# A hybrid decoder layer on one core: a second plain feature tile ahead of the block products, and the token sums on VectorE alone

## The chip, the cores and the metric

The kernel runs on one core of a Trainium2 chip. The metric is the device time of one execution in microseconds (us); the kernel before takes 1684.22 us, the median of three runs between 1683.53 and 1684.87. The engines are named as in the profile: PE is TensorE, PEld its weight load, DVE VectorE, ACT ScalarE, POOL GpSimd, and SP the engine whose queue issues the DMAs.

## What is computed

One decoder layer on 1024 tokens of width 1024 (16 learned tokens are put in front and dropped at the end). Three mixers (window attention, forgetting attention, a gated recurrence) are gated, summed and projected; then comes a gated feed-forward part, which is what the change touches:

```python
u = rms_norm(x, norm_ffn)
gate_ff, up_ff = jnp.split(u @ w_ffn_in, 2, axis=-1)      # 1024 x (2 x 2816)
h = x + (jax.nn.silu(gate_ff) * up_ff) @ w_ffn_out        # 2816 x 1024
return rms_norm(h, norm_final)[:, 16:]
```

All of it is float32.

## The kernel before

**Number form.** Every float32 operand of a matmul is held as two tiles, a high part (rounded by ACT, `split`, L118) and the rest (subtracted by DVE, L119). A product is three matmuls: high by high, high by rest, rest by high (`mm3`, L150).

**The feed-forward part** has 22 feature tiles of 128 columns (NF = 22, NJ = 11), taken in pairs j and j + 11. A plain tile (`swiglu_plain`) multiplies its gate and its up weights with both halves of the tokens: 2 x 2 products of 8 contraction steps, each of three matmuls of 512 columns, 96 matmuls. A block tile (`swiglu`) treats gate and up weights by contraction halves as the 2 x 2 blocks a11, a12, a21, a22, and the tokens by contraction and token halves as b11 to b22, and needs seven block products in place of eight, 7 x 12 = 84 matmuls. Their second operands are b11, b21, b22 and four sums of token blocks, t1 to t4, which `combine()` makes once: t2 is the second operand of a block tile's third product, t1 of the fourth, t3 of the fifth, t4 of the seventh. The first and second products need no sum. The first operands are sums of weight blocks, made on POOL (L900, L903) and split by ACT and DVE; the sixth needs such a sum too.

In the kernel before, feature tile 0 is plain and the other 21 are block tiles. PE's order is: plain tile 0; block tile 11; then the pairs 1 and 12, 2 and 13, up to 10 and 21. `combine()` works in pieces of 512 columns: of four pieces k, two are made by DVE and two by POOL (`e = pool if k > 1 else dve`), in tiles of the tag "c". For each pair `combine_w` makes sums of the second weight matrix and `combine_a` sums of the activations, all on POOL, and these are written to device memory.

**The second product** (`product2`) reads these back (tiles "raw"), splits them into "ab" tiles, and forms the 1024 x 1024 result of 7 block products with 11 contraction steps each, 12 matmuls a step. The "ab" tiles are a ring of 15 in one memory pool that lies over memory of the first product.

**Order.** Each engine works through its own list in order. A scheduler of the framework makes these lists from the program: it moves instructions of one engine past each other where the data allow it, and it places a tile when the memory under it is free. A DMA on SP's queue that waits holds up those behind it.

Of the kernel before, what the change touches and what calls it, by code (L numbers as in the profile page):

```python
# [46 lines left out]
def f32(ap):  # L47
    return ap.bitcast(F32)
# [3 lines left out]
def hybrid_block(ctx, tc, h_in, w_in, w_v0, w_v1, w_bd, par, rows, gains, relt, onehot,  # L52
# [852 lines left out]
    with tc.tile_pool(name="r5", bufs=1, side="right", reuse_waits="tile") as r5:  # L905
# [37 lines left out]
        def swiglu(f, w, bb):  # L943

            (a11, a12), (a21, a22) = w
            b11, b21, b22, t1, t2, t3, t4 = bb
            p1, p2, p5 = mm_bank(f"_s{f}"), sc_bank(f"_s{f}"), tr_bank(f"_s{f}")
            g0, g1, u1 = (t5("c", 8) for _ in range(3))
            s0, s1 = (t5("a", 6) for _ in range(2))
            s2 = t5("s2", 2)  # L950
            product(p1, operand(wp, "wh", 2, a11), b11)
            act.activation(g0, p1, AF.Copy)  # L952
            product(p2, operand(wp, "wl", 2, a12), b21)
            add(dve, g0, p2, g0)
            act.activation(s0, g0, AF.Sigmoid)
            dve.tensor_tensor(s0, g0, s0, ALU.mult)
            sub(pool, a21, a11, a21)
            sub(pool, s2, a22, a21)
            product(p1, operand(r5, "ar", 3, s2), t2, False)
            act.activation(g1, p1, AF.Copy)  # L960
            add(pool, a11, s2, a11)
            product(p5, operand(r5, "ar", 3, a11), t1)
            act.activation(u1, p5, AF.Copy)
            product(p1, operand(r5, "ar", 3, a21), t3, False)
            add(dve, u1, p1, u1)
            sub(pool, a12, a12, s2)
            product(p5, operand(wp, "wh", 2, a12), b22, False)
            add(dve, g1, p5, g1)
            act.activation(s1, g1, AF.Sigmoid)
            dve.tensor_tensor(s1, g1, s1, ALU.mult)  # L970
            dve.tensor_tensor(s1, u1, s1, ALU.mult)
            product(p1, operand(wp, "wl", 2, a22), t4, False)
            dve.tensor_tensor(s0, p1, s0, ALU.mult)
            return [s0, s1]

        def combine():

            b11, b21 = u2[0][:2], u2[0][2:]
            b12, b22 = u2[1][:2], u2[1][2:]
            t3 = [pair_tile(r5, bufs=4) for _ in range(2)]  # L980
            t2, t1 = ([pair_tile(mp) for _ in range(2)] for _ in range(2))
            parts = lambda b, k: [f32(x[:, k % 2]) for x in b[k // 2]]
            into = lambda t, k, v: split(*(x[:, k % 2] for x in t[k // 2]), v)
            v2 = {}
            for k in (0, 2, 1, 3):
                e = pool if k > 1 else dve
                v3, v2[k] = t5("c", 8), t5("c", 8)
                for v, x, y in zip((v3, v2[k]), parts(b22, k), parts(b12, k)):
                    sub(e, v, x, y)
                add(e, v3, v3, v2[k])  # L990
                for x, y in zip((v3, v2[k]), parts(b11, k)):
                    add(e, v2[k], x, y)
                into(t2, k, v2[k])
                into(t3, k, v3)
            t4 = [pair_tile(mp) for _ in range(2)]
            for t, b in ((t1, b22), (t4, b21)):
                for k in (0, 2, 1, 3):
                    e = pool if k > 1 else dve
                    v = t5("c", 8)
                    h, l = parts(b, k)  # L1000
                    sub(e, v, h, v2[k])
                    add(e, v, v, l)
                    into(t, k, v)
            return b11, b21, b22, t1, t2, t3, t4

        def spill(i, j, x):
# [2 lines left out]
        def combine_w(j):  # L1009

            raws = []
            for i in range(2):
                raw = t5("fo", 2, D)
                dma(raw, w_fo[(j + NJ * i) * P:(j + NJ * i + 1) * P])
                raws += halves(raw)
            b11, b12, b21, b22 = raws
            t2 = t5("t2", 1)
            sub(pool, b12, b22, b12)
            add(pool, t2, b12, b11)
            sub(pool, b11, b22, t2)  # L1020
# [3 lines left out]

        def combine_a(j, a11, a21, a12, a22):

            s2 = t5("t2", 1)
            spill(1, j, a12)
            spill(6, j, a22)
            sub(pool, a21, a11, a21)  # L1030
# [3 lines left out]
            for i, x in ((2, s2), (3, a11), (4, a21), (5, a12)):  # L1034
                spill(i, j, x)

        for j in range(NJ):
            if j == 0:
                first = swiglu_plain(0)
                ws = fetch_fi(NJ, 0)  # L1040
                bb = combine()
            else:
                first = swiglu(j, fetch_fi(j, 1), bb)
                ws = fetch_fi(j + NJ, 0)
            spill(0, j, first[0])
            combine_w(j)
            combine_a(j, *first, *swiglu(j + NJ, ws, bb))
    ctx4.close()

    with (tc.tile_pool(name="ring", bufs=1, side="right", reuse_waits="tile") as rr,
          tc.tile_pool(name="r6", bufs=1, side="right", reuse_waits="tile") as r6):
        def h_tile(tt, half):
            t = r6.tile([P, 512], F32, name=f"h{tt}{half}")
# [3 lines left out]
        def right_operand(i, j):  # L1059
# [2 lines left out]
            row, half = {0: (j, 0), 1: (j + NJ, 0), 5: (j + NJ, 1)}[i]  # L1062
            return w_fo[row * P:(row + 1) * P, 512 * half:512 * half + 512]

        def operands(i, j):

            raw = wp.tile([P, 2, 512], F32, tag=("wr", "wh", "wl")[j % 3], bufs=2, name=nm("raw"))
            dma(raw[:, 0], asp[i][j])
            dma(raw[:, 1], right_operand(i, j))
            t = rr.tile([P, 2, 2, 512], F32R, tag="ab", bufs=15, name=nm("ab"))  # L1070
            split(t[:, 0], t[:, 1], raw)
            return t[:, 0], t[:, 1]

# [144 lines left out]
```

## Time and profile before

| | |
|---|---|
| median of three runs | 1684.22 us |
| profiled execution, its time | 1683.39 us |
| its span (first to last instruction) | 1681.6 us |
| PE busy | 1628.9 us, 97% |
| DVE busy | 1003.4 us, 60% |
| ACT busy | 766.0 us, 46% |
| POOL busy | 463.8 us, 28% |

PE is the engine that works nearly all the time, so a microsecond counts if PE waits in it, or if its clock is low. The profile tells for each instruction how long the engine had been idle before it and what ended that; a group can be asked for by stretch of time. Times of PE instructions overlap (they are pipelined), so the step from one start to the next is the price of one. "Granted clock" is the share of 2.4 GHz that PE was given: 1.00 is that, 0.50 is 1.2 GHz.

### The profile page before, as it was taken

What the parts mean: (1) busy time and instruction counts of PE and PEld (TensorE: products, weight loads), DVE (VectorE), ACT (ScalarE), POOL (GpSimd) and SP (SyncE); (2) the same over time, 40 slices, a digit from 0 to 9 for tenths busy, and PEclk for the clock granted to TensorE, in tenths of its full rate; (3) what the DMA queues carried; (4) which work ended last, traced back from release to release, by engine and by line L of the source; (5) the groups of instructions that cost most, each with busy time, mean ns of one, the idle gap of its engine ahead of it and who ended that gap; (6) DMA issues with size and microseconds to landing.
All of it is one profiled execution on the core that took longest, in us unless ns stands there. A gap on an engine that the chain in (4) does not pass through costs nothing.

```text
span 1681.6 us, 22693 instructions
## 1 busy us (share of the span) xinstructions
PE 1628.9 (97%) x8147; PEld 1372.5 (82%) x8147; DVE 1003.4 (60%) x1815; ACT 766.0 (46%) x1413; POOL 463.8 (28%) x363
## 2 busy tenths in 40 slices
PE   7999999999999999999999995899999999999998
PEld 6898888888888888888887884688888888788886
DVE  6566566554666667532357448866666666657544
ACT  6455465554556555533345433433333333346342
POOL 2111011011122122100234007666666566300000
PEclk9999999999999999999999998899999999999999
DMA  7122342213413233159645213244444444499532
GB/s 268 55 97 92 138 135 95 96 61 117 126 64 120 83 126 97 62 176 328 197 155 189 100 63 125 98 165 157 165 167 144 145 155 158 149 358 325 192 122 100
DMA packets 110880, 242.48 MB, mean 144 GB/s; under 512 B 11944, under 2 KB 23544, under 8 KB 110512
## 3 DMA queue, kind: packets, MB, share of 16 engines
q1 hardware_dynamic: 110768, 241.04, 42.2%
q8 instruction: 64, 1.05, 0.3%
q14 instruction: 48, 0.39, 0.1%
HBM read 163.45 MB, written 72.21 MB: 140 GB/s over the span
## 4 chain that ended last, share of the span: by engine, by line
PE 80%; DVE 7%; issue 4%; DMA 4%; ACT 3%; POOL 2%; SPq 0%; POOLq 0%; DVEq 0%; ACTq 0%
PE mm_w L150 23%; PE mm_s L150 13%; PE tr_s L150 7%; PE mm_br L150 5%; PE mm_wo L150 5%; PE mm_x L1082 4%; PE sc_s L150 4%; PE ob L547 3%; PE tr L558 3%; PE tr_y L1082 3%; PE sc_y L1082 3%; PE mm_v L150 2%; PE ob_x L1082 1%; PE sc L632 1%; PE sc L633 1%
## 5 line engine op out<-in xcount | busy, mean ns | idle before, releaser
L150 PE MATMUL mm_w<-uh,wh 128*128 128x512 f32 (+2 forms) x744 | 292.6, 393 | 0.0
L150 PE MATMUL mm_w<-uh,wl 128*128 128x512 f32 (+2 forms) x744 | 280.6, 377 | 0.0
L150 PE MATMUL mm_w<-ul,wh 128*128 128x512 f32 (+2 forms) x744 | 280.0, 376 | 0.0
L150 PEld LDWEIGHTS mm_w<-uh,wl 128*128 128x128 f32 x744 | 140.0, 188 | 25.6
L150 PEld LDWEIGHTS mm_w<-uh,wh 128*128 128x128 f32 x744 | 140.5, 189 | 12.8
L150 PEld LDWEIGHTS mm_w<-ul,wh 128*128 128x128 f32 x744 | 140.8, 189 | 11.8
L119 DVE TENSOR_TENSOR ab<-raw,ab 128x1024 fp32r<-128x1024 f32 x77 | 95.9, 1262 | 62.6 <-ACT ab L118 60.2
L150 PE MATMUL mm_s<-pt,ar 128*128 128x512 f32 x504 | 121.3, 389 | 1.7 <-ACT c L952 1.7
L118 ACT ACTIVATE ab<-raw 128x1024 fp32r<-128x1024 f32 x77 | 80.9, 1059 | 88.4 <-DMA raw<-w_fo_dram 29.2
L150 PE MATMUL mm_br<-o,wh 128*128 128x512 f32 x384 | 118.6, 390 | 0.0
L118 ACT ACTIVATE wh<-wr 128x1024 fp32r<-128x1024 f32 (+1 forms) x85 | 71.7, 845 | 97.1 <-PE mm_w L150 50.6
L119 DVE TENSOR_TENSOR pl<-tr,ph 128x384 fp32r<-128x384 f32 (+2 forms) x160 | 87.4, 555 | 47.3 <-ACT ph L118 43.2
L150 PEld LDWEIGHTS mm_s<-pt,ar 128*128 128x128 f32 x504 | 94.5, 188 | 21.6 <-ACT c L952 2.1
L118 ACT ACTIVATE ph<-tr 128x384 fp32r<-128x384 f32 (+2 forms) x160 | 76.9, 486 | 53.1 <-PE tr L558 51.0
L119 DVE TENSOR_TENSOR wl<-wr,wh 128x1024 fp32r<-128x1024 f32 x43 | 53.3, 1239 | 72.2 <-ACT wh L118 71.9
L648 POOL TENSOR_SCALAR s<-s,sm 128x144 f32<-128x144 f32 (+3 forms) x64 | 48.6, 761 | 172.1 <-DVE sm L647 144.1
L150 PEld LDWEIGHTS mm_br<-o,wh 128*128 128x128 f32 x384 | 72.0, 188 | 15.3 <-ACT wh L118 0.3
L150 PE MATMUL mm_s<-pt,wh 128*128 128x512 f32 x252 | 63.4, 401 | 18.6 <-ACT wh L118 12.7
L558 PE MATMUL tr<-ident,s 128*128 128x128 f32 x480 | 79.6, 274 | 1.2 <-POOL s L596 0.6
L150 PE MATMUL mm_wo<-woh,hl 128*128 128x512 f32 x256 | 79.1, 390 | 0.0
L150 PE MATMUL mm_br<-o,wl 128*128 128x512 f32 x192 | 75.3, 392 | 1.8 <-DVE wl L119 1.6
L558 PEld LDWEIGHTS tr<-ident,s 128*128 128x128 f32 x480 | 59.1, 140 | 18.3 <-DVE pl L119 3.4
(256 smaller groups left out, 3715.8 us busy)
## 6 DMA issues: line engine op xcount, KB each, us to landing
wr<-w_in_dram SPq DMA_DIRECT2D x45, 512.0 KB, 3.6
wr<-w_fi_dram SPq DMA_DIRECT2D x44, 512.0 KB, 4.2
raw<-asp SPq DMA_DIRECT2D x77, 256.0 KB, 3.9
asp<-a SPq DMA_DIRECT2D x66, 256.0 KB, 2.9
gz<-z SPq DMA_DIRECT2D x48, 256.0 KB, 2.1
o<-osp SPq DMA_DIRECT2D x24, 512.0 KB, 5.3
sg<-gz SPq DMA_DIRECT2D x48, 256.0 KB, 3.4
fo<-w_fo_dram SPq DMA_DIRECT2D x22, 512.0 KB, 4.3
```

The source lines that it names most:

```text
L118: act.activation(hi, src, AF.Copy)
L119: i = dve.tensor_tensor(lo, src, f32(hi), ALU.subtract)
L150: pe.matmul(ps, a, b, start=first and i == 0, stop=i == n - 1, skip_group_check=not first)
L547: pe.matmul(ob[:, q0:q0 + b - a], vt[:, c], x[:, a:b], start=count == 0, stop=count == n_mm - 1, skip_group_check=True)
L558: pe.transpose(tb[:, col:col + P], src, ident)
L632: pe.matmul(sc[:, :n], qs, kh[:, k0:k0 + n], start=True, stop=False)
L633: pe.matmul(sc[:, :n], qs, kl[:, k0:k0 + n], start=False, stop=True)
L648: pool.tensor_scalar(s[:, :nk], s[:, :nk], den, 1.0, ALU.mult, ALU.mult)
L1082: pe.matmul(banks[x], a[:, 0, q], b[:, 1], start=first and j == 0 and c == 0, stop=j == NJ - 1 and c % 3 == 2, skip_group_check=True)
```

## The change

1. For j = 0 both tiles of the pair, 0 and 11, are plain, and stand ahead of `combine()` in the program. The first block tile is tile 1.
2. `combine()` works on whole tiles of 1024 columns, on DVE alone. Its temporaries take the four slots of "fo" (4 KB each), which the rows of the second weight matrix use later ("fo" had two slots); "c" has six slots, not eight. The sum tile "t2" of `combine_w` and `combine_a` moves from one slot to the two of "z".
3. From j = 1 on, the weights of the first tile of a pair are loaded into the pool "wstream" and those of the second into the pool "r5"; before, it was the other way round.
4. The ring of "ab" tiles becomes two pools: four tiles ("ring0") and ten ("ring1"), 14 in all.

```diff
-            g0, g1, u1 = (t5("c", 8) for _ in range(3))
+            g0, g1, u1 = (t5("c", 6) for _ in range(3))
...
-            for k in (0, 2, 1, 3):
-                e = pool if k > 1 else dve
-                v3, v2[k] = t5("c", 8), t5("c", 8)
-                for v, x, y in zip((v3, v2[k]), parts(b22, k), parts(b12, k)):
-                    sub(e, v, x, y)
-                add(e, v3, v3, v2[k])
-                for x, y in zip((v3, v2[k]), parts(b11, k)):
-                    add(e, v2[k], x, y)
-                into(t2, k, v2[k])
-                into(t3, k, v3)
+            temp = lambda: t5("fo", 4, D).rearrange("p (k t) -> p k t", k=2)
+            v2 = []
+            for i in range(2):
+                v3 = temp()
+                v2.append(temp())
+                for v, x, y in zip((v3, v2[i]), b22[i], b12[i]):
+                    sub(dve, v, f32(x), f32(y))
+                add(dve, v3, v3, v2[i])
+                for x, y in zip((v3, v2[i]), b11[i]):
+                    add(dve, v2[i], x, f32(y))
+                split(*t2[i], v2[i])
+                split(*t3[i], v3)
...
-                for k in (0, 2, 1, 3):
-                    e = pool if k > 1 else dve
-                    v = t5("c", 8)
-                    h, l = parts(b, k)
-                    sub(e, v, h, v2[k])
-                    add(e, v, v, l)
-                    into(t, k, v)
+                for i in range(2):
+                    v = temp()
+                    sub(dve, v, f32(b[i][0]), v2[i])
+                    add(dve, v, v, f32(b[i][1]))
+                    split(*t[i], v)
...
-                first = swiglu_plain(0)
-                ws = fetch_fi(NJ, 0)
+                first, second = swiglu_plain(0), swiglu_plain(NJ)
                 bb = combine()
+                spill(0, j, first[0])
             else:
-                first = swiglu(j, fetch_fi(j, 1), bb)
-                ws = fetch_fi(j + NJ, 0)
-            spill(0, j, first[0])
+                first = swiglu(j, fetch_fi(j, 0), bb)
+                spill(0, j, first[0])
+                second = swiglu(j + NJ, fetch_fi(j + NJ, 1), bb)
             combine_w(j)
-            combine_a(j, *first, *swiglu(j + NJ, ws, bb))
+            combine_a(j, *first, *second)
...
-    with (tc.tile_pool(name="ring", bufs=1, side="right", reuse_waits="tile") as rr,
+    with (tc.tile_pool(name="ring0", bufs=4, side="right", reuse_waits="tile") as r7,
+          tc.tile_pool(name="ring1", bufs=10, side="right", reuse_waits="tile") as r8,
...
-            t = rr.tile([P, 2, 2, 512], F32R, tag="ab", bufs=15, name=nm("ab"))
+            pl = r7 if ring[0] % 14 < 4 else r8
+            ring[0] += 1
+            t = pl.tile([P, 2, 2, 512], F32R, tag="ab", name=nm("ab"))
```

What this does to the engines' lists, at three places.

**DVE, where the first block tile's first operand is split.** "pt" are tiles of tokens and of their sums, "c" and (after) "fo" the temporaries of the sums, "wh" and "wl" first operands of a block tile, "a" the gated result. Before:

```order
L119 TENSOR_TENSOR wh_9988<-wr_9861,wh_9988 128x512
L119 TENSOR_TENSOR pt_9874<-c_9925,pt_9873 128x512
L903 TENSOR_TENSOR c_9935<-c_9935,pt_9358 128x512
L930 TENSOR_TENSOR a_9857<-mm_u_1743_9808,a_9857 128x512
L119 TENSOR_TENSOR pt_9876<-c_9930,pt_9875 128x512
L119 TENSOR_TENSOR pt_9874<-c_9935,pt_9873 128x512
L119 TENSOR_TENSOR pt_9876<-c_9940,pt_9875 128x512
L900 TENSOR_TENSOR c_9945<-pt_8985,c_9878 128x512
L900 TENSOR_TENSOR c_9955<-pt_8985,c_9900 128x512
```

After, the split of "wh" for tile 1 stands here, ahead of the splits of t4:

```order
L900 TENSOR_TENSOR fo_10034<-pt_8987,fo_10005 128x1024
L119 TENSOR_TENSOR pt_9992<-fo_10024,pt_9991 128x1024
L903 TENSOR_TENSOR fo_10034<-fo_10034,pt_8988 128x1024
L929 TENSOR_TENSOR a_9977<-mm_g_1754_9927,a_9977 128x512
L119 TENSOR_TENSOR wh_10077<-wr_10064,wh_10077 128x512
L119 TENSOR_TENSOR pt_10016<-fo_10029,pt_10015 128x1024
L119 TENSOR_TENSOR pt_10018<-fo_10034,pt_10017 128x1024
L119 TENSOR_TENSOR wl_10093<-wr_10064,wl_10093 128x512
L119 TENSOR_TENSOR ar_10113<-s_1795_10076,ar_10113 128x512
```

Before, 13 of DVE's instructions of 512 columns on the sums came after the split of the first "wh". Now only the two splits of t4 do; the other 24 instructions of `combine()`, 1024 columns wide, and the two splits of tile 11's weights stand ahead of it, from the last tiles of the tokens on.

**POOL, from the first weight sum on.** "wr" and "s" are weight blocks and their sums, "fo" and "t" those of the second matrix. Before:

```order
L900 TENSOR_TENSOR wr_9863<-wr_9861,wr_9863 128x512
L900 TENSOR_TENSOR s_1790_9987<-wr_9863 128x512
L900 TENSOR_TENSOR c_9888<-pt_9359,pt_9355 128x512
L900 TENSOR_TENSOR c_9889<-pt_9360,pt_9356 128x512
L903 TENSOR_TENSOR c_9888<-c_9888,c_9889 128x512
L903 TENSOR_TENSOR c_9889<-c_9888,pt_8983 128x512
L900 TENSOR_TENSOR fo_9966<-fo_9968,fo_9966 128x512
L903 TENSOR_TENSOR c_9889<-c_9889,pt_8984 128x512
L903 TENSOR_TENSOR t_1781_9970<-fo_9966 128x512
L900 TENSOR_TENSOR fo_9966<-fo_9968,t_1781_9970 128x512
L900 TENSOR_TENSOR fo_9968<-fo_9968,t_1781_9970 128x512
```

After:

```order
L900 TENSOR_TENSOR wr_10201<-wr_10199,wr_10201 128x512
L900 TENSOR_TENSOR a_9857<-a_9803,a_9857 128x512
L900 TENSOR_TENSOR wr_10066<-wr_10064,wr_10066 128x512
L900 TENSOR_TENSOR s_1795_10076<-wr_10066 128x512
L900 TENSOR_TENSOR s_1813_10211<-wr_10201 128x512
L903 TENSOR_TENSOR wr_10064<-s_1795_10076,wr_10064 128x512
L900 TENSOR_TENSOR fo_10040<-fo_10042,fo_10040 128x512
L903 TENSOR_TENSOR t_1783_10044<-fo_10040 128x512
L900 TENSOR_TENSOR fo_10040<-fo_10042,t_1783_10044 128x512
L900 TENSOR_TENSOR fo_10042<-fo_10042,t_1783_10044 128x512
L900 TENSOR_TENSOR wr_10064<-wr_10064,s_1795_10076 128x512
```

No sum of tokens is left on POOL. Five instructions stand ahead of the addition `wr_10064<-s_1795_10076,wr_10064`, which overwrites a block that the split of "wh" (above) reads.

**ACT, at the end of the first product.** "ab" are operands of the second product; L952 to L969 belong to the last block tile. Before:

```order
L952 ACTIVATE c_12912<-mm_s_2182_12909 128x512
L955 ACTIVATE a_12915<-c_12912 128x512
L960 ACTIVATE c_12913<-mm_s_2182_12909 128x512
L963 ACTIVATE c_12914<-tr_s_2184_12911 128x512
L969 ACTIVATE a_12916<-c_12913 128x512
L118 ACTIVATE ab_13071<-raw_13068 128x1024
```

After:

```order
L952 ACTIVATE c_12843<-mm_s_2165_12840 128x512
L118 ACTIVATE ab_13018<-raw_13015 128x1024
L955 ACTIVATE a_12846<-c_12843 128x512
L118 ACTIVATE ab_13036<-raw_13033 128x1024
L960 ACTIVATE c_12844<-mm_s_2165_12840 128x512
L118 ACTIVATE ab_13054<-raw_13051 128x1024
L118 ACTIVATE ab_13072<-raw_13069 128x1024
L963 ACTIVATE c_12845<-tr_s_2167_12842 128x512
L969 ACTIVATE a_12847<-c_12844 128x512
```

Four "ab" tiles are now rounded among the last block tile's instructions and not behind the last of them; DVE's list has their four subtractions at the same place.

On SP's queue one load per pair moves: the second half of the weights of the next pair's first tile stood ahead of the last write of `combine_a` and of three writes of `combine_w`, and now stands behind them.

## Rows read from the trace of the kernel before

**Rows 1.** Page: PE over the span, and the granted clock in 40 slices.

```profile
PE 1628.9 (97%) x8147; PEld 1372.5 (82%) x8147; DVE 1003.4 (60%) x1815; ACT 766.0 (46%) x1413; POOL 463.8 (28%) x363
PEclk9999999999999999999999998899999999999999
```

**Rows 2.** Three of the four longest waits of PE: total us, times, longest.

```profile
PE mm_s L150 <- ACT wh L118: 12.7, 1, 12.7
...
PE mm_s L150 <- DVE wh L119: 5.9, 1, 5.9
PE sc_s L150 <- DVE wl L119: 5.4, 1, 5.4
```

**Rows 3.** Timeline of PE, 1030 to 1082: start us, us, instruction, idle before.

```profile
1030.70 0.39 PE L150 MATMUL mm_u<-pt,wl 128*128 128x512 f32 x1
1043.84 1.22 PE L150 MATMUL mm_s<-pt,wh 128*128 128x512 f32 x2 [12.74 <-ACT wh L118]
...
1064.03 4.63 PE L150 MATMUL sc_s<-pt,wl 128*128 128x512 f32 x10 [5.40 <-DVE wl L119]
...
1078.94 2.88 PE L150 MATMUL mm_s<-pt,wl 128*128 128x512 f32 x12
1081.66 2.43 PE L150 MATMUL mm_s<-pt,wh 128*128 128x512 f32 x10
```

**Rows 4.** Stretches: length, busy us (count) of PE, PEld, DVE, ACT, POOL; clock; DMA.

```profile
1031.00:1043.90 12.90, 0.16 (x2) 0.07 (x1) 7.42 (x6) 2.42 (x5) 12.66 (x10) 0.63 0.29 101
...
1051.00:1055.20 4.20, 4.20 (x11) 3.33 (x12) 4.20 (x5) 2.63 (x5) 2.92 (x2) 0.54 0.00 0
...
1081.70:1462.00 380.30, 380.30 (x1679) 314.93 (x1678) 245.88 (x275) 140.70 (x236) 232.21 (x153) 1.00 0.46 157
```

**Rows 5.** Timeline of DVE, a split of 1024 columns and the next.

```profile
918.15 1.21 DVE L119 TENSOR_TENSOR wl<-wr,wh 128x1024 fp32r<-128x1024 f32 x1
919.28 0.68 DVE L119 TENSOR_TENSOR hl<-sg,hl 128x512 fp32r<-128x512 f32 x1
```

**Rows 6.** Timeline of DVE, token tiles, sums beside POOL, and splits without it.

```profile
1012.25 1.14 DVE L124 SCALAR_TENSOR_TENSOR pt<-tr,part,pt 128x128 fp32r<-128x128 f32 x3 [1.21 <-ACT pt L123]
...
1020.16 1.77 DVE L119 TENSOR_TENSOR pt<-c,pt 128x512 fp32r<-128x512 f32 x1
1021.86 1.77 DVE L903 TENSOR_TENSOR c<-c,pt 128x512 f32<-128x512 f32 x1
...
1071.70 0.69 DVE L119 TENSOR_TENSOR wl<-wr,wl 128x512 fp32r<-128x512 f32 x1
1072.31 0.69 DVE L119 TENSOR_TENSOR wh<-wr,wh 128x512 fp32r<-128x512 f32 x1
```

**Rows 7.** Timeline of POOL, beside DVE's sums, and while DVE waits.

```profile
1021.35 1.74 POOL L900 TENSOR_TENSOR fo<-fo,fo 128x512 f32<-128x512 f32 x1
...
1036.65 1.26 POOL L903 TENSOR_TENSOR c<-c,c 128x512 f32<-128x512 f32 x1
```

**Rows 8.** Page: splits of 1024 columns, DVE and ACT, mean ns of one.

```profile
L119 DVE TENSOR_TENSOR ab<-raw,ab 128x1024 fp32r<-128x1024 f32 x77 | 95.9, 1262 | 62.6 <-ACT ab L118 60.2
...
L118 ACT ACTIVATE ab<-raw 128x1024 fp32r<-128x1024 f32 x77 | 80.9, 1059 | 88.4 <-DMA raw<-w_fo_dram 29.2
```

**Rows 9.** DMA issues, 940 to 1080: KB each, median us to landing.

```profile
wr<-w_fi_dram SPq DMA_DIRECT2D x4, 512.0 KB, 4.9
```

**Rows 10.** Timeline of PE, start of the second product, and 30 us on.

```profile
1464.83 1.20 PE L1082 MATMUL sc_y<-ab 128*128 128x512 f32 x4 [2.21 <-DVE ab L119]
...
1495.19 2.11 PE L1082 MATMUL mm_x<-ab 128*128 128x512 f32 x8 [0.36 <-DVE ab L119]
```

**Rows 11.** Timeline of DVE at the start of the second product.

```profile
1462.81 8.70 DVE L119 TENSOR_TENSOR ab<-raw,ab 128x1024 fp32r<-128x1024 f32 x5
```

**Rows 12.** Timeline of SP's queue in the first product, one pair of tiles.

```profile
1123.08 0.38 SPq L58 DMA_DIRECT2D wr<-w_fi_dram  x1
...
1129.77 2.02 SPq L58 DMA_DIRECT2D bsp<-fo  x2
```

More of the change, by code (lines that the diff above doesn't have):

```diff
@@ L981, in combine @@
             t2, t1 = ([pair_tile(mp) for _ in range(2)] for _ in range(2))
-            parts = lambda b, k: [f32(x[:, k % 2]) for x in b[k // 2]]
-            into = lambda t, k, v: split(*(x[:, k % 2] for x in t[k // 2]), v)
-            v2 = {}
-            for k in (0, 2, 1, 3):
-                e = pool if k > 1 else dve
-                v3, v2[k] = t5("c", 8), t5("c", 8)
-                for v, x, y in zip((v3, v2[k]), parts(b22, k), parts(b12, k)):
-                    sub(e, v, x, y)
-                add(e, v3, v3, v2[k])
-                for x, y in zip((v3, v2[k]), parts(b11, k)):
-                    add(e, v2[k], x, y)
-                into(t2, k, v2[k])
-                into(t3, k, v3)
+            temp = lambda: t5("fo", 4, D).rearrange("p (k t) -> p k t", k=2)
[10 more added lines that the diff above has]
+                split(*t3[i], v3)
             t4 = [pair_tile(mp) for _ in range(2)]
             for t, b in ((t1, b22), (t4, b21)):
-                for k in (0, 2, 1, 3):
-                    e = pool if k > 1 else dve
-                    v = t5("c", 8)
-                    h, l = parts(b, k)
-                    sub(e, v, h, v2[k])
-                    add(e, v, v, l)
-                    into(t, k, v)
+                for i in range(2):
[3 more added lines that the diff above has]
+                    split(*t[i], v)
             return b11, b21, b22, t1, t2, t3, t4
@@ L1012, in combine_w @@
             for i in range(2):
-                raw = t5("fo", 2, D)
+                raw = t5("fo", 4, D)
                 dma(raw, w_fo[(j + NJ * i) * P:(j + NJ * i + 1) * P])
@@ L1016, in combine_w @@
             b11, b12, b21, b22 = raws
-            t2 = t5("t2", 1)
+            t2 = zp.tile([P, 512], F32, tag="z", bufs=2, name=nm("t2"))
             sub(pool, b12, b22, b12)
@@ L1025, in combine_a @@
         def combine_a(j, a11, a21, a12, a22):
-            s2 = t5("t2", 1)
+            s2 = zp.tile([P, 512], F32, tag="z", bufs=2, name=nm("t2"))
             spill(1, j, a12)
@@ L1063, in right_operand @@
             return w_fo[row * P:(row + 1) * P, 512 * half:512 * half + 512]
+        ring = [0]
         def operands(i, j):
```

## Prediction

> **What bounds the kernel now.** I read the page first: PE is busy for 97% of the span [rows 1], so a gain can come only from PE's waits, from a low clock, or from fewer matmuls. The granted clock falls below full in the 25th and 26th of the 40 slices [rows 1], 1009 to 1093 us. The list of PE's waits [rows 2] names three long ones there, 12.7, 5.9 and 5.4 us, all for first operands of a block tile. The timeline [rows 3] shows where: the plain tile's last matmul starts at 1030.70, and the next tile, a block tile, only gets going at 1064. In the hole the clock falls to half and stays there for a while: the matmuls of 1051.0 to 1055.2 have a granted 0.54 [rows 4], and the ten from 1064.03 on take 4.63 us [rows 3]. What holds PE up is the making of the token sums: POOL is busy for 12.66 of the 12.90 us of the first wait [rows 4], and DVE's list has the sums ahead of the splits that PE wants.
>
> After that PE runs without a wait to 1462 us, 380.30 of 380.30 us busy at full clock [rows 4]. There it waits once more, 2.2 us, for the first "ab" of the second product, and 0.4 us at 1495 [rows 10].
>
> **Part 1: the second plain tile takes the place of a block tile.** A block product of 12 matmuls takes 2.72 us (1078.94 to 1081.66 [rows 3]), so a matmul is 0.227 us. The plain tile 0 ends at 1030.70 + 0.23 = 1030.93. In the kernel before, block tile 11 ends at 1081.66, where tile 1 starts [rows 3]: 50.7 us for a tile whose 84 matmuls are worth 19.0 us. The other 31.7 us are waits and half clock. Now plain tile 11 takes 96 x 0.227 = 21.8 us, to 1052.7, if its weights are there, and the 20 block tiles behind it are the same as before. So the change gives 50.7 - 21.8 = 28.9 us, less what tile 1 now waits, G.
>
> The weights of tile 11: its gate weights go into the slots of tile 0's, which PE reads last at 1025.5 (one product of 24 matmuls before the end). ACT takes 1.06 and DVE 1.13 us more [rows 5, 8], so they are there at 1027.9, and the up weights, by the same count from 1030.9, at 1033.6. PE wants them at 1030.9 and 1036.4. About 3 us of cover each, which the two POOL instructions in that stretch (priced below) don't use up: nothing.
>
> **Part 2: when tile 1 can start.** Its first product needs no sum, only its split "wh", but that stands on DVE behind 24 of the 26 instructions of the sums. DVE begins with the last token tiles at 1012.25 [rows 6]. Up to "wh" come 8 token splits at 0.35 us (three take 1.14, ends overlapping [rows 6]), 26 instructions of 1024 columns (24 of sums, 2 of weights) at 1.13 (918.15 to 919.28 [rows 5]), 7 gate products of 512 at 0.60 (the step of 512 columns without POOL [rows 6]) and "wh" itself at 0.60: 2.8 + 29.4 + 4.2 + 0.6 = 37.0. With 0.5 us of waiting in between (DVE reaches the up product of tile 0's first half before PE has ended it, at 1020.3) "wh" would be ready at 1049.8, 2.9 us ahead of PE's 1052.7.
>
> POOL takes this away. Beside POOL, a DVE instruction with both operands in SBUF takes a step of 1.70 and not 0.60 (1020.16 to 1021.86 [rows 6]), and POOL's own go to 1.74 us, where one needs 1.26 while DVE waits [rows 7]: the two take turns, and each POOL instruction costs DVE 1.10 us. Five stand ahead of "wh" on POOL (order above), and the sixth waits for "wh". The third to fifth need the second half of tile 1's weights, whose load stands on SP behind the write of POOL's second; by a load's 4.9 us [rows 9] they run at about 1041 to 1046, well ahead of "wh". So 5 x 1.10 = 5.5, less 0.5 that falls into DVE's own wait: "wh" at 1054.8, and PE waits 2.1 us.
>
> The second product's "wl" comes behind t4's two splits: 1054.8 + 2 x 1.13 + 0.6 = 1057.7, against PE's 1054.8 + 2.7 = 1057.5. With one or two POOL instructions in between (+1.1 or 2.2) the wait is 1.3 to 2.4; I take 1.7, nearer to one, since POOL must wait for the load of its next. From the third product on PE needs one split in 2.72 us, which DVE makes in 1.7 even beside POOL; the sixth waits for a POOL sum behind the four of the second matrix, 5 x 1.7 = 8.5 us after their load lands at about 1057, then ACT and DVE: 1068 against PE's 1070. G = 3.8 us. Neither wait is longer than the 2.2 us before the second product [rows 10], after which the matmuls ran at full clock; so none is added for the clock.
>
> The bounds of G: below, 0 (POOL's instructions fall where DVE waits). Above: each POOL instruction costs its whole 1.74 [rows 7], and a wide one on DVE its mean of 1.26 [rows 8], 5 x 1.74 + 26 x 0.13 = 12.1, "wh" at 1061.9, a wait of 9.2; the clock then falls as before, ten matmuls at 0.42 (4.2 us [rows 4]) and not 0.227, + 2.0; and 2.4 for "wl": 13.6. I take a value near the lower rows since the step of 1.70 was read in the same kind of instructions.
>
> The Trainium skill's page "SBUF — State Buffer", section "Who interferes with whom", says that a VectorE instruction with two SBUF inputs and a GpSimd instruction that reads SBUF block each other by an exclusive lock for the whole instruction. The rows show the blocking, at 1.10 us; with POOL's whole 1.26 in its place G would be 0.8 higher. The page "Perfetto Trace Analysis", section "Optimizing Scalar/DVE Operations", says that breaking instructions up can help where VectorE is not saturated but makes others wait, which speaks against sums of 1024 columns. Here a wide one costs 1.13 against 2 x 0.60, so going back to halves would cost DVE 26 x 0.07 = 1.8 us, and the plain tile covers the later start.
>
> **Part 3: the second product's start.** The first "ab" were split behind the last block tile's last instruction, from 1462.81 on, five in 8.70 us [rows 11]; now the order has four of them among that tile's instructions, the first behind L952, which reads the tile's first product, 6 x 2.72 = 16 us before its end. So the 2.2 us go. What is late next is the fifth, behind the last block tile's end as the first was; it is wanted 4 x 2.72 = 10.9 us later. The 0.4 us at 1495 may stay: the loads there are issued in the same order. I take 2.4, between 0 (the loads come no earlier) and 2.6. A ring of 14 in place of 15 still holds 14 x 2.72 = 38 us of work: nothing. "c" with six slots holds two block tiles: nothing.
>
> **The sum.** Against the profiled execution: 1683.4 - 28.9 + 3.8 - 2.4 = 1655.9; its time is 0.8 us under the median of the runs, so **1656.7**.
>
> **Rivals.**
>
> *DVE becomes the bound.* The upper bound of G, 13.6, or a second block tile that waits too, since the DVE work that POOL had is now all in one list: 1656.7 + 9.8 = 1666.5, and up to 1675 with one more wait of that size. For it: DVE has no idle time in the list of part 2 beyond 0.5 us. Against it: PE gives DVE 21.8 us more than before. Chance 12%.
>
> *The first product starves later, and the kernel is slower.* On SP's queue one load of 512 KB per pair moves behind four writes: from 1123.08 to about 1131.8 [rows 12], 8.7 us later. It is for tile 3, which begins four tiles of 7 x 2.72 = 19.0 us after 1081.66, at 1157.8, and is wanted first in its third product, at 1163. Landing (4.9 [rows 9]), two POOL sums (3.5), ACT and DVE (2.5) bring 1131.8 to 1143, so some 19 us are left. It decides only from 19 us of further delay, if the four slots of "fo" hold the queue up as well. Each pair would then wait; at 4 us for ten pairs, 1656.7 + 40 = 1697. Chance 4%.
>
> *The sums end last all the same.* If the scheduler's order left tile 1 behind all of the sums, G would be some 5 and the time 1658; that is inside the forecast's range, and the order shows that only t4 is behind.
>
> **How the numbers follow.** Forecast (1651.5 to 1663): 82%. DVE the bound (1663 to 1676): 12%. Starving (above 1687): 4%. No clear difference: 2%. The range: below, G = 0 and the whole 2.6 give 1652.7, and 1 us for the spread of the runs; above, the upper bound of G: **1651.5 to 1666.5**. About 0.2%, 3.4 us, is what a measurement of this kernel can tell from no change: faster 94%, same 2%, slower 4%.
>
> **What would show it.** Right: PE without a wait from 1008 to about 1052.7, a clock of 1.00 there, tile 1's first matmul at 1054 to 1057, one more wait of 1 to 2.5 us for "wl", none from then on; the second product's first matmuls without a wait. Wrong: waits in tile 11 for its weights; a wait as long as the 5.4 us before, with matmuls at half clock after it; waits of PE in any later block tile; no POOL at work beside DVE before 1050, which would put G at 0.

## The result and the profile after

The changed kernel takes 1662.65 us (median of four runs, 1662.29 to 1663.59) against 1684.55 (1683.53 to 1685.96): a ratio of 0.987, 95% interval 0.9853 to 0.9887. The forecast of 1656.7 had the direction and the place; the time lies inside its range and 6.0 us above the forecast. Below are PE and its granted clock, and PE's three waits in the changed part (us in total, times, longest), which answer [rows 1] and [rows 2]. The profiled execution has a span of 1660.5 us and took 1662.29.

```profile
PE 1630.2 (98%) x8159; PEld 1375.1 (83%) x8159; DVE 999.4 (60%) x1799; ACT 760.7 (46%) x1397; POOL 433.1 (26%) x341
PEclk9999999999999999999999999899999999999999
```

```profile
PE mm_s L150 <- ACT c L952: 3.7, 1, 3.7
PE sc_s L150 <- DVE wl L119: 2.0, 1, 2.0
...
PE mm_s L150 <- DVE wh L119: 0.9, 1, 0.9
```

One of the two low slices is gone, the waits of 12.7, 5.9 and 5.4 us too. There are shorter ones for the same two first operands, and one of 3.7 us for ACT's copy L952. That kind is not new: in the kernel before, PE waited 1.66 us for the same copy in tile 11 (its timeline):

```profile
1057.89 0.73 PE L150 MATMUL mm_s<-pt,ar 128*128 128x512 f32 x2 [1.66 <-ACT c L952]
```

The timeline of PE, from the end of tile 11 to the start of tile 12 (answers [rows 3]), and then the stretches (length, busy us of PE, PEld, DVE, ACT, POOL, granted clock; they answer [rows 4]):

```profile
1052.82 0.61 PE L150 MATMUL mm_s<-pt,wh 128*128 128x512 f32 x2
1054.33 2.56 PE L150 MATMUL mm_s<-pt,wh 128*128 128x512 f32 x10 [0.90 <-DVE wh L119]
1056.73 0.61 PE L150 MATMUL sc_s<-pt,wl 128*128 128x512 f32 x2
1059.37 3.57 PE L150 MATMUL sc_s<-pt,wl 128*128 128x512 f32 x10 [2.02 <-DVE wl L119]
1066.68 4.96 PE L150 MATMUL mm_s<-pt,ar 128*128 128x512 f32 x12 [3.75 <-ACT c L952]
1071.48 2.88 PE L150 MATMUL tr_s<-pt,ar 128*128 128x512 f32 x12
...
1082.36 2.88 PE L150 MATMUL mm_s<-pt,wh 128*128 128x512 f32 x12
```

```profile
1031.00:1052.80 21.80, 21.80 (x97) 18.05 (x97) 21.23 (x18) 8.29 (x11) 12.98 (x4) 1.00 0.24 82
...
1061.00:1062.80 1.80, 1.80 (x5) 1.00 (x3) 1.80 (x4) 0.00 (x0) 1.80 (x2) 0.50 0.38 146
1062.80:1066.70 3.90, 0.15 (x2) 0.02 (x1) 2.08 (x2) 1.18 (x3) 3.90 (x3) 0.50 0.70 269
1066.70:1071.50 4.80, 4.80 (x13) 3.80 (x14) 4.80 (x5) 1.21 (x3) 4.09 (x4) 0.56 0.40 157
...
1082.00:1441.00 359.00, 359.00 (x1586) 297.26 (x1585) 244.97 (x264) 135.57 (x225) 217.33 (x145) 1.00 0.46 161
```

Tile 11 runs without a wait at full clock, and from 1082 to 1441 PE is busy all the time. Tile 1 takes 1082.36 - 1052.82 = 29.54 us for 84 matmuls worth 19.04: G is **10.5**, not 3.8. It is the wait for "wh" (the first product takes 1.2 us too long), 2.0 for "wl", 3.75 for L952, and 3.5 of half clock (1.4 in the second product, 2.1 in the third, which takes 4.80 us and not 2.72). The second product of the layer begins without a wait (answers [rows 10]; before, then after):

```profile
1462.00 0.61 PE L1082 MATMUL sc_y<-ab 128*128 128x512 f32 x2
...
1444.12 1.52 PE L1086 MATMUL sc_y<-ab 128*128 128x512 f32 x6
```

So 1462.00 - 1444.12 = 17.9 us, all at the tiles 11 and 1, and 3.2 behind it make the 21.1 us between the spans of 1681.6 and 1660.5.

Why ACT was late with L952: the timelines of ACT and then of POOL (start us, us, instruction, idle before).

```profile
1057.65 0.61 ACT L118 ACTIVATE wl<-wr 128x512 fp32r<-128x512 f32 x1
1065.52 0.63 ACT L118 ACTIVATE wh<-wr 128x512 fp32r<-128x512 f32 x1 [7.25 <-POOL wr L900]
1066.05 0.58 ACT L952 ACTIVATE c<-mm_s 128x512 f32<-128x512 f32 x1
```

```profile
1033.42 6.74 POOL L900 TENSOR_TENSOR a<-a,a 128x512 f32<-128x512 f32 x1 [16.69 <-DVE a L930]
...
1054.49 2.07 POOL L903 TENSOR_TENSOR wr<-s,wr 128x512 f32<-128x512 f32 x1 [3.64 <-ACT pt L118]
1056.52 2.25 POOL L900 TENSOR_TENSOR fo<-fo,fo 128x512 f32<-128x512 f32 x1
1058.84 1.61 POOL L903 TENSOR_TENSOR t<-fo 128x512 f32<-128x512 f32 x1
1060.54 3.28 POOL L900 TENSOR_TENSOR fo<-fo,t 128x512 f32<-128x512 f32 x2
1063.78 1.71 POOL L900 TENSOR_TENSOR wr<-wr,s 128x512 f32<-128x512 f32 x1
```

The third product adds to the bank of the first, so it must wait until L952 has copied the first one out. The bank had been full since 1057. But on ACT's list the rounding of the sixth first operand stands ahead of L952, and that waited 7.25 us for POOL, which made the four sums of `combine_w(0)` first. PE was held up by an operand that it would want three products later.

### The profile page after: what moved, and what is told of

Read it like the earlier page. It is cut to its first block, busy times and chain, and to the rows that moved or that the text cites. A ratio compares the mean times of both kernels' runs of the same rounds, so it can differ in the third digit from the quotient of the medians.

```text
span 1660.5 us, 22597 instructions
## 1 busy us (share of the span) xinstructions
PE 1630.2 (98%) x8159; PEld 1375.1 (83%) x8159; DVE 999.4 (60%) x1799; ACT 760.7 (46%) x1397; POOL 433.1 (26%) x341
## 4 chain that ended last, share of the span: by engine, by line
PE 87%; DVE 4%; issue 4%; ACT 2%; POOL 1%; DMA 1%; SPq 0%; DVEq 0%; POOLq 0%; ACTq 0%
PE mm_w L150 26%; PE mm_s L150 13%; PE tr_s L150 7%; PE mm_br L150 6%; PE mm_wo L150 5%; PE mm_x L1086 4%; PE tr_y L1086 4%; PE sc_y L1086 4%; PE ob L547 3%; PE sc_s L150 3%; PE tr L558 3%; PE mm_v L150 2%; PE ob_x L1086 1%; PE mm_g L150 1%; PE mm_u L150 1%
## 5 line engine op out<-in xcount | busy, mean ns | idle before, releaser
L150 PEld LDWEIGHTS mm_w<-uh,wh 128*128 128x128 f32 x744 | 140.4, 189 | 12.7
L118 ACT ACTIVATE ab<-raw 128x1024 fp32r<-128x1024 f32 x77 | 80.9, 1059 | 94.7 <-PE ob_x L1086 23.4
L150 PE MATMUL mm_s<-pt,ar 128*128 128x512 f32 x480 | 117.4, 394 | 3.7 <-ACT c L952 3.7
L1086 PE MATMUL mm_x<-ab 128*128 128x512 f32 x297 | 72.7, 389 | 0.0
```

What stands on the lines that cost most here:

```text
L118: act.activation(hi, src, AF.Copy)
L150: pe.matmul(ps, a, b, start=first and i == 0, stop=i == n - 1, skip_group_check=not first)
L1086: pe.matmul(banks[x], a[:, 0, q], b[:, 1], start=first and j == 0 and c == 0, stop=j == NJ - 1 and c % 3 == 2, skip_group_check=True)
```

## The experiments

Times are medians of four or five runs. "Tile 1" is the time from tile 1's first matmul to tile 12's, worth 19.0 us.

| kernel | time us | ratio to before, 95% | tile 1 | waits of PE behind tile 1 |
|---|---|---|---|---|
| changed | 1662.65 | 0.9853 to 0.9887 | 29.5 | none |
| e1 sixth operand later | 1662.23 | 0.9849 to 0.9878 | 25.2 | 2.4 in tile 12 |
| e2 combine_w(0) later | 1660.35 | 0.9838 to 0.9867 | 27.3 | none |
| e8 t4 later | 1664.55 | 0.9863 to 0.9896 | 25.1 | 4.1 in tile 12 |
| e10 sum first | 1662.52 | 0.9855 to 0.9884 | 28.0 | 0.6 |
| e6 half width | 1664.19 | 0.9864 to 0.9893 | 31.8 | none |
| e12 eight POOL sums later | 1666.88 | 0.9878 to 0.9911 | 23.0 | 9.0 in tile 12 |
| e11 the same and DVE's order | 1660.84 | 0.9842 to 0.9871 | 19.3 | 1.9 and 3.6 in tile 12 |
| e14 POOL's sums spread | **1651.33** | 0.9790 to 0.9817 | 19.5 | none |
| e15 the same without DVE's order | 1656.05 | 0.9819 to 0.9846 | 23.0 | none |
| e3 one ring | 1666.16 | 0.9877 to 0.9907 | | |
| e4 old sums | 1672.76 | 0.9914 to 0.9943 | | |
| e5 one plain tile | 1671.04 | 0.9903 to 0.9936 | | |

### What each part is worth: each undone alone

```diff
# e3: the ab tiles in one pool again
+            t = rr.tile([P, 2, 2, 512], F32R, tag="ab", bufs=15, name=nm("ab"))
# e4: combine() as before the change, "c" with 8 slots, "fo" with 2
# e5: tile 11 a block tile
-                first, second = swiglu_plain(0), swiglu_plain(NJ)
+                first = swiglu_plain(0)
+                ws = fetch_fi(NJ, 1)
                 bb = combine()
                 spill(0, j, first[0])
+                second = swiglu(NJ, ws, bb)
```

> The changed kernel, with the ring of ab tiles of the second product in one pool of 15 as before (part 3 of the sum undone), all else as changed. Theory A (the own slots for four of them are what took the wait at the start of the second product): PE waits 2.2 us again for the first ab there, and 0.4 us some 30 us later: 1665.0 to 1665.6, 2.4 to 2.9 above the changed kernel. Theory B (the loads come earlier in any case because the slots of the first product's pools are freed in another order): within 0.7 us of the changed kernel.

> The changed kernel with two plain tiles, but combine() as before: pieces of 512 columns, two by DVE and two by POOL, in tiles of the tag c. Theory A (who makes the sums hardly matters once a second plain tile covers them): the time is within 3 us of the changed kernel, 1660 to 1665.5. Theory B (POOL's half is the late half, and POOL's own sums for the weights stand behind it): tile 1's third to fifth operands come later than 1066, PE waits some 4 to 10 us more in tile 1, 1666 to 1673.

> The changed kernel with one plain tile, so that tile 11 is a block tile behind tile 0 as before, but with the sums on DVE alone in instructions of 1024 columns. Theory A (the second plain tile is the gain, since it fills the time that the sums take): PE waits from 1031 to about 1052 for wh, and tile 11 ends where tile 1 ends in the changed kernel, so the time is one block tile above it, 1662.6 + 19.0 = 1681.7 (1678 to 1685). Theory B (the quicker sums are a good part of the gain by themselves): 1672 or less.

Measured: +3.5, +10.1 and +8.4 us, together 22.0, as much as the change brought (21.9). No single one is "the" change. That they are independent is not shown: no run undoes two of them, nor the exchange of the two weight pools alone. Theory A held for the ring: its waits of 2.2 and 0.4 us are back, though the time is 0.6 us above its range. For the other two it fell, and the times lie in theory B's ranges. But with the old sums PE loses its time in another place than B said: the second plain tile itself is held up. Its weights' rounding stands on ACT behind a wait of 11.17 us for POOL's half of the sums, and PE waits 11.9 us in tile 11. Tile 1 starts 19.2 us later (1072.02) and then needs 21.0 us, not 29.5 (waits of PE, then ACT, with the old sums):

```profile
PE mm_g L150 <- ACT wh L118: 11.9, 1, 11.9
```

```profile
1037.40 1.15 ACT L118 ACTIVATE pt<-c 128x512 fp32r<-128x512 f32 x2 [11.17 <-POOL c L903]
...
1042.63 1.04 ACT L118 ACTIVATE wh<-wr 128x1024 fp32r<-128x1024 f32 x1
```

With one plain tile, "wh" was ready at 1042.6 and not at 1054, since tile 11's weights and gate products were not on DVE's list, 20 and not 24 instructions of the sums stood ahead of it, and POOL got no instruction in between (last section). My 1681.7 had carried the changed kernel's 1054 over to a kernel with another list.

### The wait in tile 1: four changes of order

```diff
# e1 (and in e8, e10): the sixth operand behind the copy L963
+                with tc.issue_after(u1_copy.ins):
+                    sixth = operand(wp, "wh", 2, a12)
# e2 (and in e10): combine_w(0) behind tile 12
-            combine_w(j)
+            if j:
+                combine_w(j)
             combine_a(j, *first, *second)
+            if j == 1:
+                combine_w(0)
# e8: the splits of t4 behind tile 1's fifth operand in the program
# e10: besides, on DVE the sum of the first two products ahead of
#      the splits of t4, the seventh operand and tile 12's first two
```

> Only tile 1's sixth first operand is split later: its rounding on ACT and its subtraction on DVE now stand behind the copy of the fourth product (L963), so that on ACT's list the copy of p1 (L952), for which PE waited 3.75 us, no longer stands behind a rounding that waits 7.25 us for POOL. Theory A (ACT's order cost the wait): the third product starts right behind the second, at about 1062.5 in place of 1066.68, the sixth operand is there in time (POOL's sum ends at 1065.5, wanted at about 1071), and the time falls by 3.75 to 6 us, to 1656.7 to 1659; the more, the more of the half clock goes too. Theory B (the half clock lasts to about 1071.5 whatever PE does): PE works in the 3.75 us, but at half clock, so that it gains half of that, 1.9 us: 1660.8. Theory C (DVE and POOL are late anyway, the wait goes to the fourth or fifth operand): less than 1.5 us, 1661.5 or more, with PE's waits now on DVE at L119.

> The sums of the second weight matrix for pair 0 (combine_w(0), four POOL instructions, two loads, four writes) are made behind tile 12 and not behind combine(); the order of ACT is that of the changed kernel. POOL then makes tile 1's sixth sum three instructions earlier, at about 1060.5 and not at 1065.5. Theory A (the wait of 3.75 us is ACT's, and ACT's is POOL's order): L952 runs at about 1061, PE's 3.75 us are gone, 1656.7 to 1659 as with the other order; the split wl of tile 1 may come 1 us earlier as well, since fewer POOL instructions are at work beside DVE. Theory B (half clock to about 1071.5 whatever PE does): 1660.8. Theory C (the four sums are missed elsewhere): PE waits at a later tile, or at the second product, and the time is 1662 or more.

> The sixth operand of tile 1 is split later, as in the first of these runs, and on DVE the two splits of t4, which only the seventh product reads, stand behind the operands of tile 1's third (one of them) and fifth product (the other), not ahead of its second operand; wl is then ready at about 1056 and not at 1059.3. Theory A (what tile 1 loses is the order of the lists, and the clock falls only because PE waits): the wait of 2.0 us for wl and that of 3.75 us go, only the one for wh, some 1.2 us, stays, and the clock stays at 1.00: G falls from 10.5 to 1 to 3, the time to 1652.5 to 1655.5. Theory B (the clock falls behind the plain tiles whatever waits follow): as much wait goes, but some ten us of matmuls at half clock cost up to 3.3 us: 1656 to 1658. Theory C (DVE as a whole is late, so whatever stands behind waits in its turn): the wait goes to the fourth to seventh product, 1659 or more.

> Five moves of order together, no work left out. On DVE, tile 1's first four operands (five splits in all) come first, then the sum of its first two products (the add behind L952), and only then the two splits of t4, the seventh operand and tile 12's first ones; on ACT the sixth operand stands behind the copy of the fourth product; the sums of the second weight matrix for pair 0 are made behind tile 12. Theory A (in the runs before, each freed wait came back because the next copy of p1, L960, stood on ACT behind the sigmoid L955, which waits for DVE's late add; nothing else is late): PE waits only for wh, 1.2 us, the third product starts at about 1059.5, the fifth at about 1065, tile 12 at about 1073.5, and the clock stays at 1.00: 1652.5 to 1655. Theory B (DVE and POOL together have more to do between 1050 and 1085 than PE's work there takes, so that the wait goes on to tile 12, as it did in two of the runs before): PE waits 2 to 5 us in tile 12 or in tile 1's seventh product, 1657 to 1662.

What was to move moved, every time, and most or all of the gain was given back one step on. In e1 the third product starts at 1061.49 and not at 1066.68, and tile 1 is 4.4 us shorter; but the scheduler, with one operand later, also put a weight sum of tile 12 behind other sums on POOL. ACT then waited 11.89 us for it, with L952 of tile 12 behind that, and PE 2.4 us, then twelve matmuls largely at half clock (a step of 4.45 us and not 2.72). The timeline of ACT in e1:

```profile
1081.53 0.63 ACT L118 ACTIVATE ar<-wr 128x512 fp32r<-128x512 f32 x1 [11.89 <-POOL wr L903]
```

In e2 the next copy of the bank was late: ACT (timeline) has the sigmoid L955 ahead of L960, and that waits for DVE's sum of the first two products.

```profile
1069.07 0.63 ACT L955 ACTIVATE a<-c 128x512 f32<-128x512 f32 x1 [5.77 <-DVE c L903]
1069.61 0.58 ACT L960 ACTIVATE c<-mm_s 128x512 f32<-128x512 f32 x1
```

In e8 it is the same wait, 2.87 us, with another of 4.05 us in tile 12 as in e1, and in e10, where that sum came first, the sixth operand's split on DVE, 5.52 us. So theory A, one instruction in the wrong place, fell. The times of e1 and e8 lie in theory C's ranges. That of e2 is near B's 1660.8, but without B's mechanism, since the clock was 1.00 until 1070; e10 is 0.5 us above B's range.

Two causes took the gain back. In tile 1 of e2, e8 and e10 it was DVE's time: in e10 it worked from 1050.5 to 1075.1 with a single gap of 0.15 us, and from 1055 on most instructions with two operands in SBUF took a step of 1.7 us, while POOL worked beside it (timeline of DVE in e10, the sixth operand's split behind these):

```profile
1067.13 3.44 DVE L119 TENSOR_TENSOR wl<-wr,wl 128x512 fp32r<-128x512 f32 x2
1070.50 1.74 DVE L119 TENSOR_TENSOR ar<-s,ar 128x512 fp32r<-128x512 f32 x1
```

In tile 12 of e1 and e8 it was POOL's list, through ACT's: from 1075 to 1080 DVE was idle in both runs. A different order of the same work only chose which product waits.

### Is it the width of 1024?

```diff
# e6: each sum and split of combine() in two pieces of 512, on DVE
+                    for k in range(2):
+                        sub(dve, h(v, k), f32(h(b[i][0], k)), h(v2[i], k))
```

> The sums are on DVE alone as in the changed kernel, but in instructions of 512 columns and not 1024, twice as many. Theory A (back-to-back wide instructions with both operands in SBUF keep POOL out, narrow ones let it in by turns): POOL's first instruction of this stretch, which took 6.74 us, takes 1.7 us or less, the write and the load behind it on SP's queue are issued some 5 us earlier (about 1035.5, not 1040.6), and DVE pays 1.1 us for it and for each of the three that now run earlier. DVE has 26 x 0.07 = 1.8 us more to do; wh comes at 1055 to 1058 and PE waits 2 to 5 us for it and not 1.2. Time: 1661 to 1666. Theory B (the number of instructions with SBUF operands, not their width, keeps POOL out): it takes 6 us or more again, the load is as late, and the time is 1664 to 1667.

No: POOL's instruction took 6.43 us again, in place of 6.74. "wh" came at 1057.3 and PE waited 3.8 us for it, then 4.2 us for the next copy of the bank (L960). The time, 1.5 us above the changed kernel, lies in both theories' ranges and differs by less than its uncertainty; the 6.43 us speak for theory B.

### POOL's sums paid later

```diff
# e12: tile 12's seven operands made ahead (prepare), then
+                    with tc.issue_after(last.ins):
+                        combine_w(0)
+                        combine_a(0, *plain)
# e11: besides, DVE's order as in e10, the sixth operand only behind the sum
# e14: as e11, but combine_w(0) behind pair 6, and for pairs 1 to 3
+                if 2 <= j <= 4:
+                    with tc.issue_after(last_sum[j].ins):
+                        combine_w(j - 1)
# e15: as e14, with DVE's and ACT's lists for tile 1 as in the changed kernel
```

> Only POOL's eight sums are put behind the last weight sum of tile 12; the lists of DVE and ACT are those of the changed kernel. Theory A (POOL's order is behind both the wait of ACT and DVE's slow steps): the wait of 2.0 us for wl stays, since the two splits of t4 still stand ahead of it, though it may shrink by 1.1 us; the one of 3.75 us goes, and the fifth product does not wait either: 1655 to 1659. Theory B (the order of DVE's list is what counts, as the sum of the first two products stands behind six splits there): the wait comes back for the fifth product, as in the run with the second matrix's sums moved: 1659.5 to 1662.

> POOL's sums that are not urgent (combine_a(0) and combine_w(0), eight instructions) are made behind the last weight sum of tile 12, and on DVE tile 1's operands and the sum of its first two products stand ahead of the splits of t4 and of tile 12's operands. Theory A (DVE has too much to do between 1050 and 1075 because nearly each of its instructions runs beside one of POOL, at a step of 1.7 and not 0.6; what POOL can do later must be later): with seven or eight POOL instructions fewer before 1070 DVE has some 8 us in hand, the sixth operand is there at about 1060, and nothing waits behind wh: 1651.5 to 1655.5. POOL's weight sums also come earlier, since the write that held up the load of tile 1's second half is gone from ahead of it. Theory B (POOL finds other work to do beside DVE, so that DVE's steps stay at 1.7, or the eight sums are missed by the writes and loads behind them on SP's queue): waits in tile 12 or in the pair behind it, 1658 or more.

> As the run with all orders, in which tile 1 lost nothing (12 products between 1053.46 and 1075.51 at full clock) but tiles 12 and 2 waited 1.95 and 3.61 us and ran some five us at half clock, because POOL's weight sums for tile 2 came behind eight others, at 1083.5 to 1087.3. Here POOL makes only combine_a(0) ahead of tile 2's weight sums; the sums of the second matrix for pairs 1, 2 and 3 come behind tile 2's, 3's and 4's last weight sum, and those for pair 0 behind pair 6. Theory A (POOL's own list is the last debt of the start, some 14 us of sums that may be paid later since POOL is busy for only 62% of the stretch from 1100 to 1440): no wait of more than 1 us from 1053 on, the clock stays at 1.00, and some 8.7 us less than that run: 1651 to 1654. Theory B (the debt is paid at the next place: tile 2, 13 or 3, or at the start of the second product, where sums of the second matrix come later): 1656 or more.

> POOL's sums are spread as in the run that waits no more, but the lists of DVE and ACT for tile 1 are those of the changed kernel (the splits of t4 ahead of wl, the sixth operand's rounding ahead of the copy of p1, six splits ahead of the sum of the first two products). Theory A (the order on DVE has a price of its own): as in the run with POOL's eight sums moved alone, PE waits 1.9 us for the copy of p1 and runs the third product at half clock (4.44 and not 2.72 us), and nothing waits behind that: 1651.3 + 3.6 = 1654.9, between 1653.5 and 1656.5. Theory B (POOL's order alone is enough): 1652.5 or less. Theory C (both are needed, the debt comes back at tile 12 or 2): 1658 or more.

In e11 tile 1 lost nothing: its operands were split mostly at a step of 0.6 us. But the eight POOL sums stood ahead of tile 2's weight sums, and tile 12 waited for them through the same list of ACT (timeline of ACT in e11; L970 and L972 are tile 12's copies):

```profile
1081.14 0.60 ACT L970 ACTIVATE c<-mm_s 128x512 f32<-128x512 f32 x1 [0.80 <-PE mm_s L150]
1087.33 0.63 ACT L118 ACTIVATE ar<-s 128x512 fp32r<-128x512 f32 x1 [5.58 <-POOL s L900]
1087.86 0.58 ACT L972 ACTIVATE c<-tr_s 128x512 f32<-128x512 f32 x1
```

In e12, without DVE's order, the same debt cost 9.0 us in tile 12, and its 1666.88 lies above the ranges of both theories. In e14 POOL pays it over six pairs, and theory A held: 1651.33, inside its 1651 to 1654. The stretches of e14:

```profile
1031.00:1053.00 22.00, 22.00 (x99) 18.03 (x97) 22.00 (x21) 7.33 (x10) 6.88 (x4) 1.00 0.25 82
1053.00:1100.00 47.00, 47.00 (x207) 38.59 (x206) 39.15 (x40) 20.72 (x35) 34.63 (x23) 1.00 0.44 152
1100.00:1440.00 340.00, 340.00 (x1501) 281.53 (x1500) 227.57 (x246) 124.72 (x207) 213.73 (x142) 1.00 0.49 173
1440.00:1500.00 60.00, 60.00 (x266) 49.70 (x265) 44.56 (x46) 37.66 (x42) 0.00 (x0) 1.00 0.96 340
```

PE does not wait from 1031 to 1500, and its clock stays up. That is 11.3 us below the changed kernel and 33.0 below the one before, and G is about 0.4. Without DVE's order (e15) PE waits 1.90 us for the copy of the bank and runs the third product at half clock (4.39 us): 1656.05, where theory A had 1653.5 to 1656.5. So POOL's order alone brings 6.6 us, and DVE's and ACT's order on top of it 4.7. Tile 1 shows 6.5 and 3.5 of these; the rest of the 4.7 lies ahead of it, where e14 reaches tile 1 at 1051.75 and e15 at 1054.00, and is not explained. The orders on DVE and ACT without POOL's sums spread give 0.1 (e10) and 1.8 us (e11) against the changed kernel. But against e12, from which e11 differs by these orders alone, they give 6.0: what one order is worth depends on the others.

## Why the prediction was right, and where it failed

- **The second plain tile, 50.7 - 21.8 = 28.9 us:** right, and 0.45 us too large. Tile 11 ends at 1052.8 (forecast 1052.7), at full clock, its weights in time. But the 50.7 us of the kernel before hold two matmuls of tile 1, which ran inside tile 11; [rows 3] has ten and not twelve from 1081.66 on. The timeline of before:

```profile
1068.46 0.66 PE L150 MATMUL mm_s<-pt,wh 128*128 128x512 f32 x2
```

- **Small sums:** 1025.5 + 1.06 + 1.13 is 1027.7 and not 1027.9, and from 1030.9 it is 1033.1 and not 1033.6. The weights of tile 11 came at 1028.7 and 1034.5, still ahead of PE. The cover of tile 3's load is 20 us by the prediction's own figures, not 19.
- **When "wh" and "wl" are ready:** right in the end points, 1054.28 (1054.8) and 1059.32 (about 1059, from 1057.5 + 1.7). The way there was different: three of the five POOL instructions fell at 1044.5 to 1050.9, not 1041 to 1046, because the second of the five took 6.74 us and held up the write and the load behind it on SP's queue (1040.56, where 1041 less a load's 4.9 gives about 1036):

```profile
1040.19 0.33 SPq L58 DMA_DIRECT2D asp<-a  x1
1040.56 0.43 SPq L58 DMA_DIRECT2D wr<-w_fi_dram  x1
```

- **The step that failed:** "From the third product on PE needs one split in 2.72 us, which DVE makes in 1.7 even beside POOL". The splits were indeed there: the third operand's at 1061.0. But I asked only when a product's operands are ready and not when its bank is free. The bank is copied by ACT, in ACT's order, behind a rounding that waits for POOL: 3.75 us. The order that I had read shows it; I had read it for DVE and POOL and not for ACT. The trace of before had the same wait, 1.66 us long, and I passed over it.
- **"so none is added for the clock":** wrong, 3.5 us. I argued from one wait of 2.2 us with full clock behind it [rows 10]. Here two waits, 0.9 and 2.0 us, 5 us apart, came ahead of a fall to 0.50. In e15 a single wait of 1.90 us did.
- **G = 3.8:** so mis-sized by 3.75 + 3.5 less 0.6 on the first two waits; it measured 10.5, inside the bounds of 0 and 13.6, which is why the range held. That was luck in part: the upper bound was made of 9.2 us for "wh" (1.2 came), 2.0 for the clock and 2.4 for "wl", and the wait for the bank stood in none of these.
- **The second product's start, 2.4:** the waits of 2.2 and 0.4 us are gone, and what lies behind its first matmul is 3.2 us shorter. With G 6.7 us too small and 0.45 too much for tile 11, that makes the 6.4 us between the 1655.9 of the sum and the profiled 1662.29. Undone alone the ring costs 3.5 us by the medians and 3.1 by the spans. The 0.36 us at 1495 [rows 10], which "may stay", went as well.
- **The rivals:** "DVE becomes the bound" was the nearest: its mechanism, the list that had lost POOL's help, is what e10 shows, though it stayed in one tile. The time is 0.35 us below the 1663 at which that rival's band begins. "Starves later" did not happen: 359.00 of 359.00 us busy behind tile 1.
- **The Trainium skill's page "SBUF — State Buffer", section "Who interferes with whom":** the blocking that it states decided more than the 0.8 us that I gave it, in the other direction too: POOL, and not only DVE, was kept waiting, for 6.74 us in one instruction.
- **The Trainium skill's page "Perfetto Trace Analysis", section "Optimizing Scalar/DVE Operations":** its advice is for an engine that is not saturated. DVE was busy for 21.23 of the 21.80 us of tile 11, and broken into halves (e6) the sums gained nothing.

## What to carry to other kernels

For each product ask three things, when its operands are ready, when its bank is free, and what stands ahead of the instruction that frees it on that engine's list; a rounding that waits for a slow engine, placed early, blocks the copy behind it. When a start-up is overloaded, moving a wait shows the next one: find work of the slow engines that nobody wants soon and spread it over the stretch where they have slack, and read the lists of all engines again after each move, since a scheduler moves other instructions too. Measure the parts of a change by undoing each alone, and do not take their sum for a proof that they are independent.

## What the runs showed of the hardware

**POOL can be kept out for a long time.** In the kernel before, DVE and POOL took turns at 1.70 us. Here a single POOL instruction took 6.74 us (the write of its result was issued at 1040.19, right behind its end), while DVE ran two-operand instructions in SBUF at their undisturbed step of 1.13. It ended when DVE had come to one that reads a PSUM bank (L929). In halves of 512 columns (e6) it is the same, with L929 at 1037.82 (timelines of the changed kernel's DVE, then e6's POOL):

```profile
1036.65 1.23 DVE L903 TENSOR_TENSOR fo<-fo,pt 128x1024 f32<-128x1024 f32 x1
1037.79 1.23 DVE L119 TENSOR_TENSOR pt<-fo,pt 128x1024 fp32r<-128x1024 f32 x1
1038.92 0.69 DVE L929 TENSOR_TENSOR a<-mm_g,a 128x512 f32<-128x512 f32 x1
```

```profile
1032.63 6.43 POOL L900 TENSOR_TENSOR a<-a,a 128x512 f32<-128x512 f32 x1 [15.86 <-DVE a L930]
```

With one plain tile it took 13.62 us, and DVE's step was 1.13 throughout (timelines of e5: POOL, then DVE):

```profile
1034.16 13.62 POOL L900 TENSOR_TENSOR a<-a,a 128x512 f32<-128x512 f32 x1 [13.18 <-DVE a L930]
1047.74 1.29 POOL L903 TENSOR_TENSOR wr<-s,wr 128x512 f32<-128x512 f32 x1
```

```profile
1044.82 1.22 DVE L900 TENSOR_TENSOR fo<-pt,fo 128x1024 f32<-128x1024 f32 x1
1045.95 0.68 DVE L119 TENSOR_TENSOR wl<-wr,wl 128x512 fp32r<-128x512 f32 x1
```

POOL's instruction ended 1.2 us after DVE's run did, about its own length. The Trainium skill's page "SBUF — State Buffer", section "Who interferes with whom", says that a VectorE instruction with at most one SBUF input, outside the 2-port modes, does not contend with GpSimd, which fits where POOL got in. That one engine loses through a whole run of instructions it does not say. The width does not decide it (e6, 6.43 us); what makes the two alternate in one place and not in another stays open.

**The same waits, two clocks.** In the changed kernel and in e3 the waits of 0.8 to 0.9 and 2.0 us in tile 1 were followed by a granted clock of 0.50; in e1 and e2, with waits of 0.81 and 0.95 and of 2.03 us at the same places, the clock stayed at 1.00 through 1065 (the stretches of e1, then e2):

```profile
1061.00:1065.00 4.00, 4.00 (x19) 3.30 (x19) 4.00 (x4) 0.63 (x1) 4.00 (x3) 1.00 0.65 252
1061.00:1065.00 4.00, 3.66 (x17) 2.71 (x16) 4.00 (x4) 2.16 (x4) 4.00 (x4) 1.00 0.59 223
```

In e15 a single wait of 1.90 us in tile 1 was followed by 0.50 from 1063 to 1066, while in the kernel before the 2.2 us ahead of the second product were followed by 1.00. So whether such waits cost a fall could not be told from the rows.
